# Gating's rows turned by pairs of 64-row transposes beside attention's last values, and mixing laid out by token blocks

## The chip, the cores and the metric

The kernel runs on one core of a Trainium2 chip (trn2). The metric is the device time of one execution in microseconds, as the median of three runs; beside the runs, one more execution was taken with the hardware profiler, and all rows come from it.

## What is computed

One layer of a streaming encoder for 320 tokens: 256 of a new stream ("prompt") and 64 that continue a running one ("sample"). What matters here is the gating group (gMLP) and where it stands:

```python
z = rmsnorm(x, ln_g) @ w_in                  # q, k, v and zs
a_o = attention(q, k, v)                     # 16 heads of 64, windows of chunks of 64
a = gelu(zs); u, v = a[..., :1024], rmsnorm(a[..., 1024:], g)
# mixing: 8 channel groups of 128; over blocks of 128 tokens (sample: one block of 64)
sp = einsum('gij,bnjgc->bnigc', masked(w_s), v.reshape(b, nb, 128, 8, 128)) + b_s.T[:, :, None]
s_o = u * sp                                 # gate
x = x + concat(rmsnorm(a_o), rmsnorm(s_o)) @ w_out
x = x + square(relu(rmsnorm(x) @ w_up)) @ w_down
```

The sample's normalised v rows are an output too (`sgu_v`).

## The kernel before

All activations stand transposed: channels on the 128 partitions, the 320 tokens along the free axis. Every big product runs in `products`: its weights come in tiles of 512 KB (four rows of 128 by 256 columns), ScalarE rounds a tile to `w_hi` (L115), VectorE makes the rest `w_lo` (L116), and TensorE runs 24 matmuls of 320 columns on it (L141, three for each of eight 128x128 blocks). One tile with its 24 matmuls is called a piece here; a column block of 256 of the input projection has four pieces. `w_hi` and `w_lo` have three buffers each, so ScalarE and VectorE may be up to three pieces ahead.

Work that is not a big product is put between two pieces: `between_pieces={k: f}` runs f's code after piece k, and `issue_after` with the list `narrow` (the last small matmul) sets that the next piece's matmuls follow f's on TensorE. For the rest a scheduler chooses the order on each engine; each engine then runs its own list in order and waits on semaphores.

The last column blocks of the input projection (g = 0 to 3, `u_pieces`) hold, between their pieces: attention's last three steps (`attend(10)`, `(11)`, `(12)`; each `attend` turns probabilities, computes scores, and computes the values of an earlier block, L485, in 64x64 quarters of the array), the gating rows' mean squares (`rows_norm`: three matmuls, L166, with the squares of 128 tokens as weights and one moving column; then VectorE's L169 and POOL's L171 give `rs_rows`), `by_rows` (transposes of v into rows of tokens, L553, evicted by ScalarE with the rows' norm as scale, L555) and `spatial` (mixing, L566 and L569, and VectorE's sums with the bias, L571 and L575, into `gv`). `gate` (L594) then multiplies by u.

The gated input v lies in `gv` (128 channels of group g, 320 tokens), its sample part also in `gvs`. Rows of tokens go to `vnat` (two blocks of the prompt, 0 and 1) and, for the sample (called the third block or t = 2 here), back into `gvs`' memory, `vnat_s`: there group 2a+x of token t stands on partition 64x + t, so that one matmul with a block-diagonal weight (`wsd`) mixes two groups.

PSUM's small banks: two of the tag `misc`, which every caller takes in rotation, and two score banks (`s_ps`, also taken as `g_ps`, `q0_ps` and so on). `banks(n)` gives the two misc banks and then the two score banks. A bank is written again only when its last reader is done. In `attend(12)` no probabilities are turned any more, so it takes two score banks and no misc bank.

Of the kernel before, what the change touches and what calls it, by code (L numbers as in the profile page):

```python
# [11 lines left out]
AF = mybir.ActivationFunctionType  # L12
ALU = mybir.AluOpType
AX = mybir.AxisListType

P = 128
T = 320
TP = 384
TT = [(0, 128), (128, 128), (256, 64)]
# [7 lines left out]
HD = 64  # L27
# [3 lines left out]
def hymba_step_kernel(ctx: ExitStack, tc: tile.TileContext, i, o):  # L31
    nc = tc.nc
# [12 lines left out]
    def misc():  # L45
        return ps_m.tile([P, 512], F32, name="misc", tag="misc")

    def score_bank(p, name="s_ps"):
        return ps_sc.tile([P, 512], F32, name=f"{name}{p}", tag=f"s{p}")
# [10 lines left out]
    cols = const.tile([P, 58], F32, name="cols")  # L60
# [14 lines left out]
    ident = const.tile([P, P], F32, name="ident")  # L75
# [6 lines left out]
    for _ in range(4):  # L82
        nc.tensor.matmul(out=warm_ps[:, 0:256], lhsT=nc.const_aps.tensor(0.0, [P, P], F32),  # L83
                         rhs=nc.const_aps.tensor(0.0, [P, 256], F32), start=True, stop=True)
# [255 lines left out]
    def banks(n, skip=0):  # L340

        return [misc() if x < 2 else score_bank(3 - x, "g_ps") for x in range(skip, skip + n)]
# [111 lines left out]
                                            op=ALU.mult).ins]  # L454
        probs[u] = s

    def attend(i):

        t, v = i - 2, i - 3
        t, v = t if 0 <= t < 10 else None, v if 0 <= v < 10 else None  # L460
        bank = [misc(), misc()] if t is not None else None
        s_ps = [score_bank(p) for p in range(2)]

        def behind(mms):
            with tc.issue_after(narrow[-1]):
                narrow.append([mm() for mm in mms][-1].ins)

        if t is not None:
            s = probs.pop(t).rearrange("x p j k -> x p (j k)")
            nk = blocks[units[t][0]][2]  # L470
            cols = ((P, 2),) if nk == HD else ((0, 0), (192, 1)) if nk == P else ((0, 0), (256, 1), (P, 2))
            behind([lambda p=p, x=x, c=c: nc.tensor.transpose(out=bank[p][:, x * P:(x + 1) * P], in_=s[:, p, c:c + P],  # L472
                                                              identity=ident) for p in range(2) for c, x in cols])
        if i < 10:
            behind([lambda: scores(i, s_ps)])
        if v is not None:
            blk_, kv = units[v]
            q0, va, vb = (blocks[blk_][x] for x in (0, 4, 5))
            hs = [slice(r * HD, (r + 1) * HD) for r in range(2)]
            side = {(r, j): bank[r][:, 384:512] if bank and j == 0 else s_ps[r][:, 384:512] if j else s_ps[r][:, 0:P]  # L480
                    for r in range(2) for j in range(2)}

            def part(r, j, p, span):
                lhsT, c = (va[j][hs[r], kv], slice(j * P, (j + 1) * P)) if span < 2 else (vb[j][hs[j], kv], slice(256, 384))
                return nc.tensor.matmul(out=side[r, j][hs[p]], lhsT=lhsT, rhs=pts[v % 2][p][hs[r], c],  # L485
                                        start=span < 2 or va is None, stop=span == 2 or vb is None or r != j)

            turns = [x for x in (0, 2, 1) if (va, va, vb)[x] is not None]
            behind([lambda r=r, p=p, x=x: part(r, 1 - r if x == 1 else r, p, x) for x in turns for r in range(2) for p in range(2)])
        if i < 10:  # L490
            softmax(i, s_ps)
        if v is not None:
            for j in range(2):
                dst = ao[:, 4 * kv + 2 * j:4 * kv + 2 * j + 2, q0:q0 + 64]
                nc.scalar.activation(out=dst, in_=side[j, j].rearrange("p (a q) -> p a q", a=2), func=AF.Copy)
                if va is not None:
                    nc.vector.tensor_tensor(out=dst, in0=dst, in1=side[1 - j, j].rearrange("p (a q) -> p a q", a=2), op=ALU.add)
        if t is not None:
            for p in range(2):
                c = slice(min(x for _, x in cols) * P, (max(x for _, x in cols) + 1) * P)  # L500
                nc.vector.tensor_copy(out=pts[t % 2][p][:, c], in_=bank[p][:, c])

    q3_ps = product(w_in, 0, KT, 768, xh, xl,
                    between_pieces={1: lambda: attend(0), 3: lambda: attend(1)})
# [39 lines left out]
    vnat_s = gvs.rearrange("p a t -> p (a t)")  # L544
    rv = []

    def by_rows(*ths):

        for (t, h), vps in zip(ths, banks(len(ths))):
            t0, n = TT[t]  # L550
            for a in range(4):
                cols = gv[:, 4 * h + a, t0:t0 + n] if t < 2 else gvs[:, 2 * a:2 * a + 2].rearrange("p x t -> p (x t)")
                mm = nc.tensor.transpose(out=vps[:, a * P:(a + 1) * P], in_=cols, identity=ident)  # L553
            dst = vnat[:, t, h * 512:(h + 1) * 512] if t < 2 else vnat_s
            nc.scalar.activation(out=dst, in_=vps, func=AF.Copy, scale=rv[0][:, t:t + 1])  # L555
        narrow.append(mm.ins)
        if ths[-1][0] == 2:
            for x in range(2):
                nc.gpsimd.dma_start(out=o["sgu_v"].rearrange("t (a x c) -> x t a c", a=4, x=2)[x],
                                    in_=vnat_s[x * HD:(x + 1) * HD].rearrange("t (a c) -> t a c", a=4))  # L560

    def spatial(*gs, skip=0):
        for g, sp_ps in zip(gs, banks(len(gs), skip)):
            cs = slice(g * P, (g + 1) * P)
            for b in range(2):
                nc.tensor.matmul(out=sp_ps[:, b * P:(b + 1) * P], lhsT=vnat[:, b, cs], rhs=wsT[:, g], start=True,  # L566
                                 stop=True)
            if g % 2 == 0:
                mm = nc.tensor.matmul(out=sp_ps[:, 256:384], lhsT=vnat_s[:, g // 2 * P:(g // 2 + 1) * P],  # L569
                                      rhs=wsd[:, g // 2], start=True, stop=True)  # L570
            nc.vector.tensor_tensor(out=gv[:, g, 0:256].rearrange("p (b i) -> p b i", b=2),  # L571
                                    in0=sp_ps[:, 0:256].rearrange("p (b i) -> p b i", b=2),
                                    in1=sgb[:, g, None, :].to_broadcast([P, 2, P]), op=ALU.add)
            if g % 2 == 0:
                nc.vector.tensor_tensor(out=gv[:, g:g + 2, 256:T], in0=sp_ps[:, 256:384].rearrange("p (x i) -> p x i", x=2),  # L575
                                        in1=sgb[:, g:g + 2, 0:HD], op=ALU.add)
        narrow.append(mm.ins)

    def rows_norm():
        rv.append(rstd_rows(acc_v, inv_1k, 4 * EPS))  # L580
# [2 lines left out]
    parts_a, rm_a = [], rstd_b("rm_a")  # L583
    u_pieces = {
        0: {1: lambda: attend(10), 3: lambda: attend(11)},
        1: {1: lambda: (rows_norm(), attend(12), by_rows((0, 0))), 2: lambda: by_rows((1, 0), (0, 1), (1, 1), (2, 0)),
            3: lambda: spatial(0, 1, 2, 3)},
        2: {1: lambda: spatial(4, 5, 6, 7)},
        3: {1: lambda: rstd(tuple(parts_a), mean_1k, EPS, rm_a)}}
    gus = {}  # L590

# [158 lines left out]
```

## Time and profile before

| what | value |
|---|---|
| median of 3 runs | 1239.58 us (1239.25 to 1239.84) |
| the profiled execution | 1239.04 us |
| its span, first to last instruction | 1237.3 us |
| TensorE matmul | 1232.8 us busy, 8666 records |
| VectorE, ScalarE, POOL | 663.6, 492.0, 114.0 us busy |
| granted TensorE clock over the span | 1.000 |
| the stage that changes | about 175.7 to 198.3 us of the span |

How to read it: PE is TensorE's matmuls, PEld its weight loads, DVE VectorE, ACT ScalarE, POOL GpSimd, SP the engine that issues loads. Matmuls are pipelined, so a record is longer than the distance to the next one: distances between starts tell what a matmul costs. A float32 matmul shows as two records, a transpose or a float32r matmul as one. In the chain, a piece stands by its end; in timelines by its start, so the two differ by a constant of 0.1 to 0.2 us.

### The profile page before, as it was taken

The page shows a single profiled execution, that of the slowest core. Times are in us where ns is not written, and L with a number is a line of the kernel's source. Part 1 is how long each engine was busy: PE and PEld are TensorE (multiplying, and loading weights), DVE is VectorE, ACT ScalarE, POOL GpSimd, SP SyncE. Part 2 cuts the span into 40 slices and gives each one's busy share as a digit, 9 for nine tenths or more (in the row PEclk, how much of TensorE's full clock was granted, in tenths as well). Part 3 has the DMA queues.
Part 4 walks back from the last instruction along what each step waited for, and adds up shares of the span by engine and source line. Part 5 has one row for each costly group of instructions (what it writes and reads, how often), then busy time and mean ns, then how long its engine had stood idle before and what let it go on. Part 6 is the DMA issues. An engine that isn't in the chain of part 4 may idle for free.

```text
span 1237.3 us, 20626 instructions
## 1 busy us (share of the span) xinstructions
PE 1232.8 (100%) x8666; PEld 1225.0 (99%) x8666; DVE 663.6 (54%) x796; ACT 492.0 (40%) x652; POOL 114.0 (9%) x139
## 2 busy tenths in 40 slices
PE   9999999999999999999999999999999999999998
PEld 9999999999999999999999999999999999999998
DVE  7877778877864444444444444444444434444343
ACT  7446566435534432333434332344432333433321
POOL 3127454102200000000000000000000000000000
PEclk9999999999999999999999999999999999999999
DMA  9753346444555444454444444455444454445540
GB/s 282 226 148 104 104 138 195 153 154 141 151 152 153 153 147 145 152 154 149 146 149 153 154 150 143 151 154 152 147 147 151 154 151 144 150 152 164 172 161 33
DMA packets 187934, 188.03 MB, mean 152 GB/s; under 512 B 7616, under 2 KB 187376, under 8 KB 187840
## 3 DMA queue, kind: packets, MB, share of 16 engines
q1 hardware_dynamic: 186544, 185.48, 48.7%
q0 software_dynamic: 864, 0.98, 0.4%
q8 instruction: 68, 1.11, 0.4%
q10 hardware_dynamic: 432, 0.24, 0.1%
q14 instruction: 26, 0.21, 0.1%
HBM read 183.10 MB, written 3.35 MB: 151 GB/s over the span
## 4 chain that ended last, share of the span: by engine, by line
PE 99%; DVE 0%; issue 0%; ACT 0%; DVEq 0%
PE acc L141 93%; PE q_ps L237 1%; PE misc L141 1%; PE acc L237 1%; PE s_ps L420 1%; PE misc L472 0%; PE misc L83 0%; PE misc L485 0%; PE s_ps L485 0%; PE g_ps L566 0%; PE misc L566 0%; PE misc L553 0%; PE misc L323 0%; ACT s L449 0%; ACT w_hi L115 0%
## 5 line engine op out<-in xcount | busy, mean ns | idle before, releaser
L116 DVE TENSOR_TENSOR w_lo<-w_raw,w_hi 128x1024 fp32r<-128x1024 f32 x332 | 416.0, 1253 | 422.7 <-ACT w_hi L115 414.1
L115 ACT ACTIVATE w_hi<-w_raw 128x1024 fp32r<-128x1024 f32 x332 | 351.8, 1060 | 670.9 <-PE acc L141 646.7
L141 PE MATMUL acc<-H2H,w_lo 128*128 128x320 f32 x1024 | 316.4, 309 | 0.0
L141 PE MATMUL acc<-H2H,w_hi 128*128 128x320 f32 x1024 | 316.4, 309 | 0.0
L141 PE MATMUL acc<-H2L,w_hi 128*128 128x320 f32 x1024 | 316.4, 309 | 0.0
L141 PE MATMUL acc<-FH,w_hi 128*128 128x320 f32 x992 | 306.5, 309 | 0.0
L141 PE MATMUL acc<-FL,w_hi 128*128 128x320 f32 x992 | 306.5, 309 | 0.0
L141 PE MATMUL acc<-FH,w_lo 128*128 128x320 f32 x992 | 306.5, 309 | 0.0
L141 PEld LDWEIGHTS acc<-H2H,w_hi 128*128 128x128 f32 x1024 | 192.2, 188 | 0.0
L141 PEld LDWEIGHTS acc<-H2L,w_hi 128*128 128x128 f32 x1024 | 192.2, 188 | 0.0
L141 PEld LDWEIGHTS acc<-H2H,w_lo 128*128 128x128 f32 x1024 | 192.2, 188 | 0.0
L141 PEld LDWEIGHTS acc<-FH,w_hi 128*128 128x128 f32 x992 | 186.2, 188 | 0.0
L141 PEld LDWEIGHTS acc<-FL,w_hi 128*128 128x128 f32 x992 | 186.2, 188 | 0.0
L141 PEld LDWEIGHTS acc<-FH,w_lo 128*128 128x128 f32 x992 | 186.2, 188 | 0.0
L141 PE MATMUL acc<-XH,w_hi 128*128 128x320 f32 x352 | 110.7, 314 | 0.0
L141 PE MATMUL acc<-XH,w_lo 128*128 128x320 f32 x352 | 108.8, 309 | 0.0
L141 PE MATMUL acc<-XL,w_hi 128*128 128x320 f32 x352 | 108.7, 309 | 0.0
L141 PEld LDWEIGHTS acc<-XH,w_hi 128*128 128x128 f32 x352 | 66.1, 188 | 3.1 <-issue 3.0
L141 PEld LDWEIGHTS acc<-XL,w_hi 128*128 128x128 f32 x352 | 66.1, 188 | 0.0
L141 PEld LDWEIGHTS acc<-XH,w_lo 128*128 128x128 f32 x352 | 66.1, 188 | 0.0
L658 DVE SCALAR_TENSOR_TENSOR tf<-acc,r 128x640 f32<-128x640 f32 x32 | 26.4, 824 | 41.8 <-PE acc L141 41.8
L673 DVE TENSOR_TENSOR xT<-xT,acc 128x640 f32<-128x640 f32 x31 | 25.5, 821 | 41.8 <-PE acc L141 41.8
(227 smaller groups left out, 1086.3 us busy)
## 6 DMA issues: line engine op xcount, KB each, us to landing
w_raw<-in_w_up SPq DMA_DIRECT2D x128, 512.0 KB
w_raw<-in_w_down SPq DMA_DIRECT2D x128, 512.0 KB
w_raw<-in_w_in SPq DMA_DIRECT2D x44, 512.0 KB
w_raw<-in_w_out SPq DMA_DIRECT2D x32, 512.0 KB
w_first<-in_w_in SPq DMA_DIRECT2D x14, 256.0 KB
out_yT<-xT SPq DMA_DIRECT2D x7, 320.0 KB
xT<-in_xT SPq DMA_DIRECT2D x8, 160.0 KB
xT<-in_xT SPq DMA_DIRECT2D x4, 320.0 KB
```

What stands on the lines that cost most here:

```text
L115: return (pin(nc.scalar.activation(out=hi, in_=raw, func=AF.Copy)).ins, pin(nc.vector.tensor_tensor(out=lo, in0=raw, in1=hi.bitcast(F32), ...
L116: pin(nc.vector.tensor_tensor(out=lo, in0=raw, in1=hi.bitcast(F32), op=ALU.subtract)).ins)
L141: mm = nc.tensor.matmul(out=out, lhsT=w_[:, k, g * P:(g + 1) * P], rhs=r_(kk), start=(kk == 0 and x == 0), stop=(kk == nk - 1 and x == 2))
L237: mm = nc.tensor.matmul(out=ps[:, 0:T], lhsT=w_[:, j, k, g * P:(g + 1) * P], rhs=r_(a + k), start=(a + k == 0 and x == 0), stop=(a + k == ...
L420: mm = nc.tensor.matmul(out=s_ps[p][x * HD:(x + 1) * HD, j * nk:(j + 1) * nk], lhsT=qT[hs, blk_, a + x], rhs=kz[hs, kv, k0:k0 + nk], start ...
L658: nc.vector.scalar_tensor_tensor(out=t, in0=ps[:, :, 0:T], scalar=0.0, in1=r2[:, None, :].to_broadcast([P, 2, T]), op0=ALU.max, op1=ALU.mult)
L673: nc.vector.tensor_tensor(out=xT[:, a, c], in0=xT[:, a, c], in1=p, op=ALU.add)
```

## The change

The diff, with what it does:

```diff
-    def attend(i):
+    def attend(i, beside=None):
...
+        if beside:
+            with tc.issue_after(narrow[-1]):
+                after = beside(s_ps)
         if i < 10:
             behind([lambda: scores(i, s_ps)])
...
+        if beside:
+            after()
...
-    def by_rows(*ths):
-        for (t, h), vps in zip(ths, banks(len(ths))):
-            t0, n = TT[t]
-            for a in range(4):
-                cols = gv[:, 4 * h + a, t0:t0 + n] if t < 2 else gvs[:, 2 * a:2 * a + 2].rearrange("p x t -> p (x t)")
-                mm = nc.tensor.transpose(out=vps[:, a * P:(a + 1) * P], in_=cols, identity=ident)
-            dst = vnat[:, t, h * 512:(h + 1) * 512] if t < 2 else vnat_s
-            nc.scalar.activation(out=dst, in_=vps, func=AF.Copy, scale=rv[0][:, t:t + 1])
+    def by_rows(t, *spans):
+        for a0, n, vps in spans:
+            for a in range(a0, a0 + n):
+                cols = gv[:, a, t * P:(t + 1) * P]
+                mm = nc.tensor.transpose(out=vps[:, (a - a0) * P:(a - a0 + 1) * P], in_=cols, identity=ident)
         narrow.append(mm.ins)
-        if ths[-1][0] == 2:
+        rows = vnat[:, t]
+        for a0, n, vps in spans:
+            nc.scalar.activation(out=rows[:, a0 * P:(a0 + n) * P], in_=vps[:, 0:n * P], func=AF.Copy, scale=rv[0][:, t:t + 1])
+
+    def by_halves(t, n, vps):
+        for a in range(n):
             for x in range(2):
...
+                hs = slice(x * HD, (x + 1) * HD)
+                cols = gv[hs, a, t * P:(t + 1) * P] if t < 2 else gvs[hs, 2 * a:2 * a + 2].rearrange("p x t -> p (x t)")
+                mm = nc.tensor.transpose(out=vps[x][:, a * HD:(a + 1) * HD], in_=cols, identity=ident[hs, hs])
+        narrow.append(mm.ins)
+        def out():
+            rows = (vnat[:, t] if t < 2 else vnat_s).rearrange("p (a x c) -> p x a c", a=n, x=2)
+            for x in range(2):
+                nc.scalar.activation(out=rows[:, x], in_=vps[x].rearrange("p (a c) -> p a c", a=n), func=AF.Copy,
+                                     scale=rv[0][:, t:t + 1])
...
+        return out
+
+    def first_rows(s_ps):
+        rows_norm()
+        outs = [by_halves(2, 4, [s_ps[x][:, P:384] for x in range(2)]), by_halves(0, 8, [misc() for _ in range(2)])]
+        return lambda: [out() for out in outs]
+
+    def sample_mix():
+        sp_ps = misc()
+        for a in range(4):
+            mm = nc.tensor.matmul(out=sp_ps[:, a * P:(a + 1) * P], lhsT=vnat_s[:, a * P:(a + 1) * P], rhs=wsd[:, a],
+                                  start=True, stop=True)
+        narrow.append(mm.ins)
+        nc.vector.tensor_tensor(out=gv[:, :, 256:T], in0=sp_ps.rearrange("p (g i) -> p g i", g=8), in1=sgb[:, :, 0:HD],
+                                op=ALU.add)
+
+    def mix():
+        for x, sp_ps in enumerate(banks(4)):
+            b, gs = x // 2, slice(x % 2 * 4, x % 2 * 4 + 4)
+            for y in range(4):
+                g = x % 2 * 4 + y
+                mm = nc.tensor.matmul(out=sp_ps[:, y * P:(y + 1) * P], lhsT=vnat[:, b, g * P:(g + 1) * P], rhs=wsT[:, g],
+                                      start=True, stop=True)
+            nc.vector.tensor_tensor(out=gv[:, gs, b * P:(b + 1) * P], in0=sp_ps.rearrange("p (g i) -> p g i", g=4),
+                                    in1=sgb[:, gs], op=ALU.add)
+        narrow.append(mm.ins)
...
     u_pieces = {
         0: {1: lambda: attend(10), 3: lambda: attend(11)},
-        1: {1: lambda: (rows_norm(), attend(12), by_rows((0, 0))), 2: lambda: by_rows((1, 0), (0, 1), (1, 1), (2, 0)),
-            3: lambda: spatial(0, 1, 2, 3)},
-        2: {1: lambda: spatial(4, 5, 6, 7)},
+        1: {1: lambda: attend(12, first_rows),
+            2: lambda: (by_rows(1, *((4 * x, 4, score_bank(x, "g_ps")) for x in range(2))), sample_mix()), 3: mix},
```

`spatial` goes. Before, attend(12) was followed by four full transposes of block 0, the next gap had sixteen (the rest of both blocks and the sample's four), and two gaps had mixing by groups. After, attend(12) has the mean squares, eight half transposes of the sample (into the free columns of the two score banks) and sixteen of block 0 (into the two misc banks) ahead of its values; the next gap has block 1's eight full transposes and the sample's mixing, the third gap all the mixing of the prompt by block and half of the groups. A half transpose takes the 64 channels on one half of the partitions; the two halves of a group go to two banks. Their evictions (`out`) come after the values' in the code. VectorE's sums are five instead of twelve. The new function's lines are L569 (half transposes), L575 (their evictions), L557 and L561 (full transposes and evictions), L592 and L595 (the sample's mixing and sum), L603 and L605 (the prompt's); attention's values (L485) are L488 there, their evictions (L495, L497) L498 and L500, and the gate (L594) is L623.

On TensorE, in the gap with attend(12), behind the three matmuls of the mean squares (the numbers at the names tell buffers of one name apart; misc_2282 is the bank of the mean squares). Before:

```order
L166 MATMUL misc_2282<-inv_1k_104,acc_v_1056 128x1 x3
L485 MATMUL s_ps0_2290<-pt1_868,kzv_465 64x128 x2
L485 MATMUL s_ps1_2291<-pt1_868,kzv_465 64x128 x2
L485 MATMUL s_ps0_2290<-pt1_868,kzv_465 64x128 x2
L485 MATMUL s_ps1_2291<-pt1_868,kzv_465 64x128 x2
L485 MATMUL s_ps0_2290<-pt1_868,kzv_465 64x128 x2
L485 MATMUL s_ps1_2291<-pt1_868,kzv_465 64x128 x2
L553 MATMUL misc_2308<-ident_89,gv_1055 128x128 x4
```

And after, from the third pair of the sample's half transposes on (two pairs stand ahead, and ahead of them the mean squares into misc_2284):

```order
L569 MATMUL s_ps0_2282<-ident_89,gvs_1057 128x64
L569 MATMUL s_ps1_2283<-ident_89,gvs_1057 128x64
L569 MATMUL s_ps0_2282<-ident_89,gvs_1057 128x64
L569 MATMUL s_ps1_2283<-ident_89,gvs_1057 128x64
L569 MATMUL misc_2300<-ident_89,gv_1055 128x64 x8
L569 MATMUL misc_2301<-ident_89,gv_1055 128x64 x8
L488 MATMUL s_ps0_2282<-pt1_868,kzv_465 64x128 x2
L488 MATMUL s_ps1_2283<-pt1_868,kzv_465 64x128 x2
```

The sample's halves alternate; block 0's do not, although the code writes them in turn: eight of the first half stand ahead of eight of the second, which write misc_2301, the bank that misc_2284 had (the tag has two). The values stand behind all of them.

On VectorE, around the reader of the mean squares (`r_rows`). Before:

```order
L524 SCALAR_TENSOR_TENSOR gu_2212<-gc_2215,z_2213 128x640
L116 TENSOR_TENSOR w_lo_2372<-w_raw_2370,w_hi_2371 128x1024
L206 SCALAR_TENSOR_TENSOR AL_2211<-ao_86,cols_82,AH_2210 128x320
L169 TENSOR_SCALAR r_rows_2286<-misc_2282 128x3
L116 TENSOR_TENSOR w_lo_2456<-w_raw_2454,w_hi_2455 128x1024
```

After:

```order
L529 SCALAR_TENSOR_TENSOR gu_2212<-gc_2215,z_2213 128x640
L116 TENSOR_TENSOR w_lo_2390<-w_raw_2388,w_hi_2389 128x1024
L206 SCALAR_TENSOR_TENSOR AL_2211<-ao_86,cols_82,AH_2210 128x320
L169 TENSOR_SCALAR r_rows_2288<-misc_2284 128x3
L116 TENSOR_TENSOR w_lo_2478<-w_raw_2476,w_hi_2477 128x1024
```

Nothing moved here: a weight half and a split of attention's output stand ahead of it in both.

On ScalarE, in the same gap, from one weight tile's high half to the next. Before:

```order
L115 ACTIVATE w_hi_2455<-w_raw_2454 128x1024
L495 ACTIVATE ao_86<-s_ps0_2290 128x2x64
L495 ACTIVATE ao_86<-s_ps1_2291 128x2x64
L555 ACTIVATE vnat_867<-misc_2308,rs_rows_2288 128x512
L115 ACTIVATE w_hi_2485<-w_raw_2484 128x1024
```

After:

```order
L115 ACTIVATE w_hi_2477<-w_raw_2476 128x1024
L575 ACTIVATE vnat_867<-misc_2300,rs_rows_2290 128x8x64
L575 ACTIVATE vnat_867<-misc_2301,rs_rows_2290 128x8x64
L498 ACTIVATE ao_86<-s_ps0_2282 128x2x64
L498 ACTIVATE ao_86<-s_ps1_2283 128x2x64
L575 ACTIVATE gvs_1057<-s_ps1_2283,rs_rows_2290 128x4x64
L575 ACTIVATE gvs_1057<-s_ps0_2282,rs_rows_2290 128x4x64
L115 ACTIVATE w_hi_2507<-w_raw_2506 128x1024
```

Block 0's evictions, which need the row norms, now stand ahead of those of attention's values, and the sample's behind them.

More of the change, by code (lines that the diff above doesn't have):

```diff
@@ L545, in hymba_step_kernel @@
     rv = []
-    def by_rows(*ths):
-        for (t, h), vps in zip(ths, banks(len(ths))):
-            t0, n = TT[t]
-            for a in range(4):
-                cols = gv[:, 4 * h + a, t0:t0 + n] if t < 2 else gvs[:, 2 * a:2 * a + 2].rearrange("p x t -> p (x t)")
-                mm = nc.tensor.transpose(out=vps[:, a * P:(a + 1) * P], in_=cols, identity=ident)
-            dst = vnat[:, t, h * 512:(h + 1) * 512] if t < 2 else vnat_s
-            nc.scalar.activation(out=dst, in_=vps, func=AF.Copy, scale=rv[0][:, t:t + 1])
-        narrow.append(mm.ins)
-        if ths[-1][0] == 2:
-            for x in range(2):
-                nc.gpsimd.dma_start(out=o["sgu_v"].rearrange("t (a x c) -> x t a c", a=4, x=2)[x],
-                                    in_=vnat_s[x * HD:(x + 1) * HD].rearrange("t (a c) -> t a c", a=4))
@@ L562, in spatial @@
[L562 to L576, printed above, removed]
+    def by_rows(t, *spans):
[3 more added lines that the diff above has]
+                mm = nc.tensor.transpose(out=vps[:, (a - a0) * P:(a - a0 + 1) * P], in_=cols, identity=ident)
+        narrow.append(mm.ins)
+        rows = vnat[:, t]
+        for a0, n, vps in spans:
+            nc.scalar.activation(out=rows[:, a0 * P:(a0 + n) * P], in_=vps[:, 0:n * P], func=AF.Copy, scale=rv[0][:, t:t + 1])
@@ new lines, in by_halves @@
+    def by_halves(t, n, vps):
+        for a in range(n):
+            for x in range(2):
+                hs = slice(x * HD, (x + 1) * HD)
[7 more added lines that the diff above has]
+                                     scale=rv[0][:, t:t + 1])
+                if t == 2 and x == 1:
+                    for y in range(2):
+                        nc.gpsimd.dma_start(out=o["sgu_v"].rearrange("t (a x c) -> x t a c", a=4, x=2)[y],
+                                            in_=vnat_s[y * HD:(y + 1) * HD].rearrange("t (a c) -> t a c", a=4))
+        return out
```

## The prediction

> **What bounds the kernel now.** I read the page's busy times, then the list of what TensorE waited for, then the chain that ended last around the change, and then the engines' timelines there.
>
> ```profile
> PE 1232.8 (100%) x8666; PEld 1225.0 (99%) x8666; DVE 663.6 (54%) x796; ACT 492.0 (40%) x652; POOL 114.0 (9%) x139
> PE 99%; DVE 0%; issue 0%; ACT 0%; DVEq 0%
> PE misc L472 <- DVE vnat L501: 0.3, 1, 0.3
> ```
>
> TensorE is busy all the time, the chain runs through it from end to end, and in the whole kernel it waits for another engine's work once, for 0.3 us. So what TensorE issues is the time, and each wait that the change gives it is added to the end in full. The chain through the stage that changes (start, us, what):
>
> ```profile
> 176.03 0.56 PE misc L166 x6
> 176.60 0.82 PE s_ps L485 x24
> 177.41 0.59 PE misc L553 x4
> 178.00 3.51 PE acc L141 x24
> 181.51 0.87 PE misc L553 x8
> 182.39 0.87 PE g_ps L553 x8
> ...
> 186.77 0.89 PE misc L566 x8
> ...
> 189.00 7.04 PE acc L141 x48
> 196.04 0.44 PE misc L566 x4
> ```
>
> L141 is the projection; between its pieces stand the sums of squares (L166), attention's last values (L485), the row transposes (L553) and the mixing (L566, L569). A full transpose takes 0.87 / 8 = 0.109 us, a mixing matmul two records of 0.89 / 8 = 0.111. A mixing group has 20 records: 189.00 - 186.77 = 2.23.
>
> **The change, costed.** First the work that is only recounted. The third block's transposes and those of block 0 leave the full form (4 + 8 = 12 of 20): -12 x 0.109 = -1.31 us. Mixing keeps 20 matmuls, 40 records in both; eight now stand with block 1's transposes, 32 in one group, at the same 0.111: 0. Instead come 24 half transposes, 64 rows in and 64 columns through. Their price is not in this trace. Lowest: two halves side by side, each half as long as a full one, 0.027 a half. Highest: each as long as a full one, 0.109. The nearest rows are the scores, which also move 64 columns from 64 rows (chain; 64, 128 and 192 columns):
>
> ```profile
> 70.79 0.39 PE s_ps L420 x16
> 78.42 0.60 PE s_ps L420 x16
> 86.47 0.81 PE s_ps L420 x16
> ```
>
> Sixteen records in four rounds of four: 64 columns more cost a round (0.60 - 0.39) / 4 = 0.053 us, which is half of 0.109. And four matmuls on different quarters do start together:
>
> ```profile
> 167.91 0.32 PE L485 MATMUL misc<-kzv 64*64 64x128 f32 x1
> ...
> 167.94 0.32 PE L485 MATMUL s_ps<-vnat,kzv 64*64 64x128 f32 x1
> ```
>
> So I take 0.055 for a half among others of the same partitions, and 0.055 for two halves of different partitions that alternate. In the order of the instructions only the third block's eight alternate (4 x 0.055 = 0.22); block 0's stand as eight of one half, then eight of the other (16 x 0.055 = 0.88). Sum for the halves: +1.10 (0.66 to 2.6).
>
> A change of array shape costs something: from the projection to the scores the starts lie 70.72 - 70.48 = 0.24 apart, where projection starts lie 3.51 / 24 = 0.15 apart.
>
> ```profile
> 70.48 0.31 PE L141 MATMUL acc<-XH,w_lo 128*128 128x320 f32 x1
> 70.72 0.46 PE L420 MATMUL s_ps<-kzv,qT 64*64 64x64 f32 x16
> ```
>
> The halves add one such change, to the values behind them: +0.09 (0 if the values share their shape, 0.18 if both ends pay).
>
> Now the wait that is new. Block 0's second eight write the `misc` bank that rows_norm's sums (L166) have just used (there are two, taken in rotation); VectorE must read that bank first (L169). Who stands ahead of L169 on VectorE, and what TensorE does meanwhile:
>
> ```profile
> 176.02 1.23 DVE L116 TENSOR_TENSOR w_lo<-w_raw,w_hi 128x1024 fp32r<-128x1024 f32 x1
> 177.16 1.16 DVE L206 SCALAR_TENSOR_TENSOR AL<-ao,cols,AH 128x320 fp32r<-128x320 f32 x1
> 178.25 0.15 DVE L169 TENSOR_SCALAR r_rows<-misc 128x3 f32<-128x3 f32 x1
> 175.87 0.72 PE L166 MATMUL misc<-inv_1k,acc_v 128*128 128x1 f32 x6
> 176.53 0.89 PE L485 MATMUL s_ps<-pt,kzv 64*64 64x128 f32 x24
> 177.34 0.66 PE L553 MATMUL misc<-ident,gv 128*128 128x128 f32 x4
> 177.76 0.39 PE L141 MATMUL acc<-XH,w_hi 128*128 128x320 f32 x1
> ```
>
> The sums are done long before VectorE gets to them; L169 ends at 178.25 + 0.15 = 178.40, and nothing ahead of it there moves with the change (the rows of VectorE are the same in both). In the kernel before nobody on TensorE asks for that bank before the transposes at 181.51, so it cost nothing. What TensorE needs to start after such a wait is in the one wait of the trace:
>
> ```profile
> 166.78 0.55 DVE L501 COPY vnat<-misc 128x384 f32<-128x384 f32 x1
> 167.47 0.52 PE L472 MATMUL misc<-ident,s 128*128 128x128 f32 x3 [0.34 <-DVE vnat L501]
> ```
>
> 167.47 - (166.78 + 0.55) = 0.14. So, by starts: halves begin at 176.53, where the values began; 0.22 and 0.44 bring 177.19; the second eight can begin at 178.40 + 0.14 = 178.54: a wait of 1.35 us. Behind it on TensorE are the values and the next projection piece. The second eight end at 178.98, the values start at 179.07 and take 177.34 - 176.53 = 0.81 as before; the projection goes on at 179.88 instead of 177.76, 2.12 later. Then block 1 has 8 transposes where 16 stood (-0.87), the third block's mixing 8 records (+0.89), the mixing 32 records where 40 stood (-0.89).
>
> 2.12 - 0.87 + 0.89 - 0.89 = **+1.25 us**; by kinds: -1.31 + 1.10 + 0.09 + 1.35 = 1.23, the same within rounding. Of the halves' own bounds only the last eight count, since the first sixteen run into the wait: at 0.027 it would be +1.03, at 0.109 +1.68.
>
> What else moves, and is hidden. ScalarE's two evictions of block 0 now stand ahead of the values' evictions (L495) and wait for POOL's power (L171):
>
> ```profile
> 178.47 1.79 POOL L171 TENSOR_TENSOR rs_rows<-r_rows,nhalf 128x3 f32<-128x3 f32 x1 [0.50 <-DVE r_rows L169]
> 179.75 0.28 ACT L495 ACTIVATE ao<-s_ps 128x128 f32<-128x128 f32 x1 [1.85 <-DVE ao L497]
> 180.30 0.69 ACT L555 ACTIVATE vnat<-misc,rs_rows 128x512 f32<-128x512 f32 x1 [0.27 <-POOL rs_rows L171]
> ```
>
> From 180.30: two of 0.69, two of 0.28, two of 256 columns at about 0.42 (between 0.28 for 128 and 0.69 for 512) end by 183.1. Block 1's transposes want these banks at 179.88 + 3.51 = 183.4, and the mixing of the third block after that: 0.3 us to spare. If that is gone, each 0.1 us of ScalarE is 0.1 us of TensorE. The output DMA on POOL's queue goes earlier, and the load queue on SP keeps its order: 0.
>
> The profiled execution took 1239.04 us (span 1237.3), so 1240.3 for it; the runs' median lies 0.54 higher, 1239.58 + 1.26 = **1240.8**.
>
> **The rivals.**
> *The halves are bound by their weight load* and cost 0.109 each. For it: L166 moves a single column and still takes 0.56 / 6 = 0.093 a record. Against it: the loads of the transposes are recorded shorter than those of L166, and nearly as short as 64-column loads (min/median/max ns):
>
> ```profile
> L553 PEld LDWEIGHTS misc<-ident,gv x12: 139/141/142, 177.3 to 182.0; 128*128 128x128 f32 x12
> L166 PEld LDWEIGHTS misc<-inv_1k,acc_v x6: 187/192/192, 175.7 to 176.3; 128*128 128x128 f32 x6
> L420 PEld LDWEIGHTS s_ps<-kzv,qT x160: 129/133/135, 70.7 to 149.9; 64*64 64x64 f32 x160
> ```
>
> The first sixteen then end by 176.53 + 1.75 = 178.28, still before 178.54; only the last eight add 8 x 0.054 = 0.43: +1.68, 1241.3. [...]
>
> *The wait does not bite.* If VectorE read the sums before L206, at 177.25, the second eight could start at 177.25 + 0.15 + 0.14 = 177.54: 1.00 us less, +0.25; if it never mattered, 1.25 - 1.35 = -0.10: 1239.5 to 1239.8. For it: L169 depends on nothing later than L166. Against it: the order puts L206 and its 1.16 us ahead.
>
> *Weight halves come late.* VectorE now waits for the whole mixing, then runs two gates in a row, and ScalarE takes their squares and copies ahead of the next w_hi. Before, this part was early by much:
>
> ```profile
> 198.27 14.08 PE acc L141 x96
> 199.06 1.37 DVE L116 TENSOR_TENSOR w_lo<-w_raw,w_hi 128x1024 fp32r<-128x1024 f32 x1
> 191.43 2.09 DVE L594 SCALAR_TENSOR_TENSOR gv<-gv,gu 128x640 f32<-128x640 f32 x1
> 193.88 0.46 ACT L509 ACTIVATE acc_s<-gv 128x320 f32<-128x320 f32 x1
> ```
>
> This w_lo is ready at 200.43 for the piece at 198.27 + 7.04 = 205.31: 4.9 us early. Now mixing ends near 179.88 + 3.51 + 1.76 + 3.51 + 3.55 = 192.2; the last sum (0.7) and the first gate (2.1) bring VectorE to 195.0, six squares and copies and a tanh at about 0.5 ScalarE to 198.5, w_hi and w_lo (1.06 and 1.37) 200.9, for the piece at 192.2 + 3 x 3.52 = 202.8: some 2 us are left. It decides if those slip; say 1.0 us on top, 1241.8.
>
> *Slower: the clock falls while TensorE waits.* The trace has a slow TensorE once, at its start: four records in 1.34 us, then 0.58.
>
> ```profile
> 4.57 1.34 PE q_ps L237 x4
> 5.91 0.58 PE acc L237 x4
> ```
>
> If 1.35 us without work brought back such a spell of 5 us at 0.58 / 1.34 of the speed, 5 x (1 - 0.43) = 2.8 us would be lost: +4.1, 1243.7. Against it: the wait at 167 is followed by no slower record. It decides where an idle spell between 0.3 and 1.35 us is enough.
>
> **How the numbers follow.** Forecast (wait of 1.35, halves at 0.055): 0.62. Load-bound halves: 0.17. No wait: 0.08. Late weights: 0.08. Clock: 0.05. A measurement of this kernel can tell about 0.2% from no change, 2.5 us. Forecast, load-bound halves, missing wait and most of late weights lie inside; the clock case and a worse lateness are slower, 0.07; nothing here gives 2.5 us back, since all 24 halves and the wait for nothing would be -1.31, so faster is 0.01, same 0.92. The range 1239.7 to 1241.9 holds the forecast, the load-bound halves (1241.3), late weights and the upper end of the missing wait.
>
> **What will show it.** Right: TensorE waits once more, some 1.3 us, its second eight halves (L569) released by L169 on VectorE; the third block's halves start in pairs; block 0's halves about 0.055 apart; the piece behind attend(12) starts near 179.9, the mixing is one group of 3.55 us, and from 200 us on every row stands 1.2 to 1.3 us later. Wrong: halves 0.11 apart (load), no wait at L569, waits of L141 for w_lo around 200 to 206, L141 records further than 0.147 apart after 178.5 (clock), or waits at L557 for ScalarE's evictions.

## The result: a wait as forecast, and a clock that was not

In 21 executions the changed kernel took 1242.08 us in the median (1240.49 to 1244.08), the kernel before 1239.6 (1238.89 to 1240.82, 21 executions): a ratio of 1.0021, 95% interval 1.0014 to 1.0027. That is +2.5 us where +1.25 was forecast, above the range's upper end of 1241.9. The median hides two groups. Nine executions list a mean granted clock of 1.000 and took 1240.49 to 1241.77; twelve list 0.999 or less and took 1241.87 to 1244.08. The profiled execution (1241.19 us, span 1239.4) is one of the first group.

Its page's busy times, and the list of what TensorE waited for (engine, line, what released it; us in total, times, longest):

```profile
PE 1233.4 (100%) x8678; PEld 1224.8 (99%) x8678; DVE 664.3 (54%) x789; ACT 491.8 (40%) x653; POOL 116.7 (9%) x139
```
```profile
PE misc L569 <- DVE r_rows L169: 1.3, 1, 1.3
...
PE misc L472 <- DVE vnat L504: 0.3, 1, 0.3
```

One wait is new, at the forecast place and from the forecast releaser. The chain round it (start us, us, what):

```profile
177.31 0.65 issue
177.96 1.15 DVE AL L206
179.12 0.08 DVE r_rows L169
179.20 0.04 issue
179.24 0.71 PE misc L569 x8
179.95 0.82 PE s_ps L488 x24
180.77 3.71 PE acc L141 x24
184.48 0.87 PE g_ps L557 x8
185.36 0.89 PE misc L592 x8
186.25 3.52 PE acc L141 x24
189.77 1.78 PE misc L603 x16
191.56 1.79 PE g_ps L603 x16
```

In the kernel before, the chain ran through TensorE all through this stage; here it leaves TensorE and runs through VectorE. The timeline shows the wait itself, and that POOL's sum of squares (L518) lies beside L206:

```profile
176.93 0.46 PE L569 MATMUL s_ps<-ident,gvs 64*128 64x64 f32 x8
...
177.23 0.66 PE L569 MATMUL misc<-ident,gv 64*128 64x64 f32 x8
...
177.74 1.03 POOL L518 TENSOR_TENSOR acc_a<-acc_a,sq 128x320 f32<-128x320 f32 x1 [2.67 <-ACT sq L517]
177.96 1.15 DVE L206 SCALAR_TENSOR_TENSOR AL<-ao,cols,AH 128x320 fp32r<-128x320 f32 x1
...
179.04 0.15 DVE L169 TENSOR_SCALAR r_rows<-misc 128x3 f32<-128x3 f32 x1
...
179.24 0.71 PE L569 MATMUL misc<-ident,gv 64*128 64x64 f32 x8 [1.35 <-DVE r_rows L169]
```

How much of a difference belongs to the changed stage can be read from two rows of each trace: the projection piece ahead of the stage, and TensorE's last record (before, then after, of both):

```profile
159.49 0.41 PE L141 MATMUL acc<-XH,w_hi 128*128 128x320 f32 x1
...
1233.69 0.31 PE L141 MATMUL misc<-FH,w_lo 128*128 128x320 f32 x1
```
```profile
159.90 0.41 PE L141 MATMUL acc<-XH,w_hi 128*128 128x320 f32 x1
...
1235.80 0.31 PE L141 MATMUL misc<-FH,w_lo 128*128 128x320 f32 x1
```

Ahead of the stage the profiled executions differ by 0.41 us, at the end by 2.11, so the stage itself costs 1.70. What differs ahead of 159 us lies ahead of the changed instructions; over all profiles below it is 0.07 to 1.18 us, a part of the scatter of the times. Behind the stage nothing more is gained or lost: from 210 us to the end each profile keeps its difference. The column "stage" below is this difference, worked out in the same way for each profile.

### The profile page after: what moved, and what is told of

It reads as the page before. It is cut to its first block, busy times and chain, and to the rows that moved or that the text cites. A ratio compares the mean times of both kernels' runs of the same rounds, so it can differ in the third digit from the quotient of the medians.

```text
span 1239.4 us, 20642 instructions
## 1 busy us (share of the span) xinstructions
PE 1233.4 (100%) x8678; PEld 1224.8 (99%) x8678; DVE 664.3 (54%) x789; ACT 491.8 (40%) x653; POOL 116.7 (9%) x139
## 3 DMA queue, kind: packets, MB, share of 16 engines
q8 instruction: 68, 1.11, 0.4%
## 4 chain that ended last, share of the span: by engine, by line
PE 96%; DMA 2%; DVE 1%; issue 1%; SPq 0%; ACT 0%; DVEq 0%; ACTq 0%
PE acc L141 93%; DMA xT<-in_xT 1%; PE misc L141 1%; PE s_ps L420 1%; SPq L110 0%; PE misc L472 0%; DVE ssq L290 0%; PE misc L488 0%; PE s_ps L488 0%; DVE w_lo L116 0%; DMA kzv<-in_cv 0%; PE g_ps L603 0%; PE misc L603 0%; ACT w_hi L115 0%; PE misc L323 0%
## 5 line engine op out<-in xcount | busy, mean ns | idle before, releaser
L116 DVE TENSOR_TENSOR w_lo<-w_raw,w_hi 128x1024 fp32r<-128x1024 f32 x332 | 417.6, 1258 | 421.2 <-ACT w_hi L115 412.6
L141 PE MATMUL acc<-H2H,w_lo 128*128 128x320 f32 x1024 | 316.4, 309 | 0.0
L141 PE MATMUL acc<-H2L,w_hi 128*128 128x320 f32 x1024 | 316.4, 309 | 0.0
L141 PE MATMUL acc<-H2H,w_hi 128*128 128x320 f32 x1024 | 316.4, 309 | 0.0
L141 PE MATMUL acc<-FH,w_hi 128*128 128x320 f32 x992 | 306.5, 309 | 0.0
L141 PE MATMUL acc<-FL,w_hi 128*128 128x320 f32 x992 | 306.5, 309 | 0.0
L141 PE MATMUL acc<-FH,w_lo 128*128 128x320 f32 x992 | 306.5, 309 | 0.0
L141 PEld LDWEIGHTS acc<-H2H,w_hi 128*128 128x128 f32 x1024 | 192.2, 188 | 0.0
L141 PEld LDWEIGHTS acc<-H2H,w_lo 128*128 128x128 f32 x1024 | 192.2, 188 | 0.0
L141 PEld LDWEIGHTS acc<-H2L,w_hi 128*128 128x128 f32 x1024 | 192.2, 188 | 0.0
L141 PEld LDWEIGHTS acc<-FH,w_hi 128*128 128x128 f32 x992 | 186.2, 188 | 0.0
L141 PEld LDWEIGHTS acc<-FL,w_hi 128*128 128x128 f32 x992 | 186.2, 188 | 0.0
L141 PEld LDWEIGHTS acc<-FH,w_lo 128*128 128x128 f32 x992 | 186.2, 188 | 0.0
L141 PE MATMUL acc<-XH,w_hi 128*128 128x320 f32 x352 | 110.6, 314 | 0.0
L141 PE MATMUL acc<-XH,w_lo 128*128 128x320 f32 x352 | 108.8, 309 | 0.0
L141 PE MATMUL acc<-XL,w_hi 128*128 128x320 f32 x352 | 108.7, 309 | 0.0
L141 PEld LDWEIGHTS acc<-XH,w_hi 128*128 128x128 f32 x352 | 66.1, 188 | 3.3 <-issue 3.0
L141 PEld LDWEIGHTS acc<-XL,w_hi 128*128 128x128 f32 x352 | 66.1, 188 | 0.0
L141 PEld LDWEIGHTS acc<-XH,w_lo 128*128 128x128 f32 x352 | 66.1, 188 | 0.0
```

What stands on the lines that cost most here:

```text
L116: pin(nc.vector.tensor_tensor(out=lo, in0=raw, in1=hi.bitcast(F32), op=ALU.subtract)).ins)
L141: mm = nc.tensor.matmul(out=out, lhsT=w_[:, k, g * P:(g + 1) * P], rhs=r_(kk), start=(kk == 0 and x == 0), stop=(kk == nk - 1 and x == 2))
```

## The experiments

Theory A: the wait at L569 is the loss, and its idleness also makes TensorE's clock fall in part of the executions, which costs them more than the wait. Theory B: the clock falls because of the halves or the mixing layout. One table has all kernels. The kernel before was run beside each: it had 1239.42 us (22 executions) beside the early sums, the overfilled wait, the kernel before with a wait and the longer wait, 1239.56 (21) beside POOL's sum later and all halves, and 1239.85 (33) beside the others. In the code cuts below, `...` stands for lines left out.

| kernel | median us (range, executions) | lists a clock under 1.000 | stage, us |
|---|---|---|---|
| changed, again | 1241.28 (1240.92 to 1243.42, 11) | 5 | 2.88 |
| sums early | 1239.51 (1238.69 to 1241.02, 11) | 0 | -0.24 |
| wait overfilled | 1242.71 (1242.29 to 1244.47, 9) | 0 | 3.16 |
| wait filled | 1241.15 (1240.73 to 1241.91, 11) | 1 | 1.82 |
| before, with a wait | 1242.97 (1241.59 to 1243.71, 8) | 5 | 3.67 |
| longer wait | 1244.40 (1243.59 to 1245.0, 5) | 5 | 5.08 |
| sums read first | 1240.22 (1239.38 to 1241.05, 11) | 0 | 0.24 |
| POOL's sum later | 1241.25 (1239.97 to 1242.67, 11) | 3 | 1.11 |
| mixing alone | 1239.81 (1238.98 to 1241.09, 11) | 1 | 0.00 |
| all halves | 1239.69 (1239.11 to 1239.91, 11) | 1 | -0.04 |

A listed 0.999 is no proof by itself: 8 of the 76 executions of the kernel before list it too. In the trace of the early sums the clock also fell when TensorE had run out of work at the very end (to 0.50 at 1236.9 us, 2.2 us behind the last matmul), which may be why. Proof is a spell in a trace: a stretch at half clock while TensorE works.

**The changed kernel again.** Nothing is edited.

> The changed kernel itself, next to the others on one chip. Theory A: two groups of times, some 1.7 to 2.0 us apart (1241.2 and 1243.1), about half of the executions in each; where the profiled execution is of the later group, a spell of 3.4 us at half clock begins within 3.4 us behind the wait's start at 177.7 us. Theory B: the same groups, the spell elsewhere.

This profile (1242.51 us) is of the later group. Windows of its trace, cut where its clock changes (from:to, length, busy us of PE, PEld, DVE, ACT, POOL with counts, granted clock, DMA share, GB/s), and its chain:

```profile
176.32:179.73 3.41, 2.46 (x36) 2.24 (x39) 3.29 (x5) 2.00 (x4) 1.72 (x2) 1.00 0.16 29
179.73:183.14 3.41, 3.41 (x31) 3.08 (x32) 0.83 (x3) 1.93 (x5) 1.09 (x1) 0.50 0.85 256
183.14:186.56 3.42, 3.42 (x27) 3.41 (x27) 0.10 (x1) 1.41 (x3) 1.31 (x2) 1.00 0.42 94
```
```profile
179.01 0.71 PE misc L569 x8
179.72 1.47 PE s_ps L488 x24
181.19 4.63 PE acc L141 x24
```

The stretch of 3.41 us that holds the wait has 3.41 - 2.46 = 0.95 us without TensorE work; the next one is granted half the clock, though TensorE works all through it, and then the clock is back. The values take 1.47 instead of 0.82, the projection piece 4.63 instead of 3.71: 1.57 us, near half of 3.41. (The stage is only 1.18 us longer than in the first profile, since the wait is 0.40 shorter.) The place is the one that theory A named. Together the 32 executions of the changed kernel have medians of 1241.13 us at clock 1.000 (15) and 1243.0 below it (17): 1.9 apart.

Why only in half of them? In the traces the recorded clock first rises 4.3 to 6.2 us into the program, and its later changes lie whole multiples of 3.413 us behind that. In the kernel before the one later change comes 1232.21 us behind the rise, in the first profile of the changed kernel 1235.63, one step of 3.41 more: 361 and 362 of them. The spell of this profile and those of two below begin 174.08 us behind it, 51 steps. Counted so (an estimate from these distances), the 51st step of the changed kernel's first profile ends at 4.50 + 174.08 = 178.58 us, in the middle of the wait:

```profile
175.17:178.58 3.41, 2.72 (x31) 2.57 (x29) 2.58 (x3) 3.38 (x5) 0.84 (x1) 1.00 0.00 0
178.58:181.99 3.41, 2.75 (x41) 2.51 (x42) 1.74 (x3) 0.89 (x2) 1.99 (x2) 1.00 0.67 171
```

That leaves 0.69 and 0.66 us of idleness in the two steps, and no spell. These two profiles fit one reading: what counts is how much of the wait lies in one step, and that shifts from execution to execution. For the other executions, which have no trace, it is not shown.

**Sums early: the wait taken away.** The sums go to unused columns of a score bank at the end of attend(11):

```diff
-        st = misc()                                     # rstd_rows takes st as an argument
...
+        if i == 11:                                     # in attend, behind the values
+            with tc.issue_after(narrow[-1]):
+                rows_norm(s_ps)                         # sums in s_ps[0][:, P:P + 4]
...
-        rows_norm()                                     # in first_rows
```

> The changed kernel, but rows_norm's sums are issued at the end of attend(11), one projection piece and more earlier, and into unused columns of a score bank, so that block 0's second eight halves find their bank free. Theory A (the wait at L569 is the loss, and it is also what makes the granted clock fall in part of the executions): no wait at the halves, all 24 halves in pairs, the stage shorter by the wait of 1.51 us and by about eight halves of 0.0625 (0.5): 1241.1 (the changed kernel's executions at clock 1.000) - 2.0 = 1239.1 us, and every execution at 1.000. Theory B (the halves or the mixing layout cost the clock, the wait does not): still about half of the executions at 0.999, these some 1.9 us later, median near 1240.5. Theory C (something else eats it: evictions or weights late once the wait is gone): 1239.6 or more at clock 1.000, with a new wait of TensorE between 178 and 206 us.

No wait, all executions at clock 1.000, and the halves run in pairs all through:

```profile
177.60 0.46 PE L572 MATMUL s_ps<-ident,gvs 64*128 64x64 f32 x8
177.90 0.66 PE L572 MATMUL misc<-ident,gv 64*128 64x64 f32 x16
```

The sixteen halves of block 0 take the 0.66 us that eight took before. The stage is 1.70 + 0.24 = 1.94 us shorter than the changed kernel's, as theory A has it (2.0). The gain of 0.24 over the kernel before shows in the stage alone: the ratio is 0.9999, interval 0.999 to 1.0008.

**The wait filled.** Twelve, then six products by the identity between the two eights:

```diff
+                if t == 0 and (x, a) == (1, 0):
+                    with tc.issue_after(mm.ins):
+                        for y in range(FILL):           # 12, then 6
+                            mm = nc.tensor.matmul(out=free[y % 2][:, 0:P], lhsT=ident, rhs=gv[:, y % 8, 0:P], start=True, stop=True)
...
```

The lines left out fix block 0's order as the changed kernel has it: eight of the first half, the products, eight of the second.

> The changed kernel, with twelve products of 128x128 by the identity between block 0's first and second eight halves, written to columns of the score banks that the values overwrite later: TensorE works through most of the 1.5 us that it waited, and starts the second eight when it did. Theory A (idleness makes the clock fall): the same times of start as in the changed kernel, all executions at clock 1.000, median 1241.2 us with a spread of about 1 us, none above 1242.3. Theory B (halves or layout cost the clock): about half of the executions at 0.999, up to 1244, median near 1242. If the twelve take longer than the wait, up to 0.2 us more in either.

> The changed kernel with six products between block 0's first and second eight halves instead of the twelve of the run before: twelve took 24 records of 0.112 = 2.7 us and overran the wait, six take 1.34 and fit into its 1.51. Theory A (idleness makes the clock fall): TensorE's starts behind the halves as in the changed kernel, no half-speed spell, every execution in one group round 1241.2 us. Theory B (halves or layout cost the clock): two groups as in the changed kernel, round 1241.2 and 1243.2, median near 1242.

Twelve were too many: they are 24 records, 2.7 us, and the stage is 1.46 us longer than the changed kernel's (3.16 against 1.70), where I had allowed for 0.2. None of the nine executions lists a clock under 1.000, but their times, up to 1244.47, can't be compared with theory A's. Six fit. The window that holds the former wait, in the second run:

```profile
176.70:180.11 3.41, 3.41 (x52) 3.15 (x55) 2.93 (x4) 1.17 (x2) 2.56 (x2) 1.00 0.43 108
```

TensorE is busy throughout, the end is as late as with the wait (stage 1.82 against 1.70), and the later group is gone: 1240.73 to 1241.91, median 1241.15, that of the changed kernel at clock 1.000 (one execution lists 0.999, at 1241.86). Halves and layout are the changed kernel's, the times of start too but for 0.1 us. Theory B falls.

**A wait in the kernel before.** No halves, the old mixing; the first four transposes are put ahead of attend(12) and into the sums' own bank:

```diff
-        for (t, h), vps in zip(ths, banks(len(ths))):
+        for (t, h), vps in zip(ths, banks(len(ths)) if len(ths) > 1 else rv[1:]):   # rv[1] is the sums' bank
...
-        1: {1: lambda: (rows_norm(), attend(12), by_rows((0, 0))),
+        1: {1: lambda: (rows_norm(), by_rows((0, 0)), attend(12)),
```

> The kernel before, with block 0's first four transposes put ahead of attend(12) and into the bank of the sums: no halves and no new mixing, only a wait for L169 that should last some 2.0 us (the sums end near 176.4, L169 near 178.4). Theory A: 1239.6 + 2.0 = 1241.6 in the executions at clock 1.000, and half or more at 0.999, some 1.9 us later, so a median of 1242.5 to 1243.6. Theory B: 1241.6 in all executions, clock 1.000.

Two executions are at 1241.6, which is the expected 2.0 us of the wait alone, and six are from 1242.64 to 1243.71; five of these six list a clock under 1.000, the lowest does not. The profiled one (1243.18, a wait of 1.8 us) is of the five:

```profile
175.50:178.91 3.41, 1.56 (x14) 1.48 (x13) 3.29 (x5) 2.62 (x4) 1.09 (x2) 1.00 0.02 7
178.91:182.33 3.42, 3.42 (x32) 2.76 (x33) 1.27 (x2) 1.24 (x3) 1.73 (x1) 0.50 0.79 223
```
```profile
178.82 1.07 PE misc L555 x4
179.90 1.49 PE s_ps L487 x24
181.38 4.17 PE acc L142 x24
```

A step with 3.41 - 1.56 = 1.85 us without TensorE work is followed by one at half clock, and four full transposes take 1.07 us where before eight took 0.87. The wait alone, without halves or the new mixing, is enough.

**A longer wait.** Three copies on VectorE read the sums ahead of L169:

```diff
+        slow = sums("slow")
+        for _ in range(3):
+            nc.vector.tensor_copy(out=slow[:, :, None], in_=st[:, 0:1, None].to_broadcast([P, T, 1]))
```

> The changed kernel, with three copies of 320 columns on VectorE that read the sums ahead of L169; a weight half of 1.2 us falls between them in VectorE's order, so that the wait at L569 grows from 1.5 to about 4 us. Theory A: the wait's own growth of 2.6 us in every execution, and the clock falls in nearly all of them: median 1241.1 + 2.6 + 2 to 4 = 1245.7 to 1247.7, with clocks of 0.997 to 0.999. Theory B (the wait costs no clock): 1241.1 + 2.6 = 1243.7 where the clock is 1.000, half of the executions at 0.999 as without it.

The wait grew less than both theories were told, to 2.3 us. The split (L209 here) took 0.55 us instead of 1.15, and the weight half ahead of it began 1.0 us earlier against TensorE than in the first profile of the changed kernel (176.09 with the piece at 160.19, against 176.82 with 159.90):

```profile
177.24 0.55 DVE L209 SCALAR_TENSOR_TENSOR AL<-ao,cols,AH 128x320 fp32r<-128x320 f32 x1
...
178.26 2.72 POOL L521 TENSOR_TENSOR acc_a<-acc_a,sq 128x320 f32<-128x320 f32 x2 [3.92 <-ACT acc_a L517]
```
```profile
175.84:179.26 3.42, 2.35 (x29) 2.20 (x27) 3.30 (x6) 2.34 (x5) 1.00 (x1) 1.00 0.17 31
179.26:182.67 3.41, 2.21 (x32) 2.09 (x32) 1.02 (x4) 0.00 (x0) 3.25 (x4) 0.50 0.85 265
182.67:186.08 3.41, 3.41 (x20) 3.12 (x13) 0.58 (x2) 2.54 (x6) 0.19 (x2) 0.50 0.06 18
186.08:189.49 3.41, 3.41 (x28) 3.40 (x28) 0.31 (x1) 1.40 (x2) 1.20 (x2) 1.00 0.37 77
```

The wait reaches into two steps (1.07 and 1.20 us idle), and two steps are at half clock. All five executions are later than any of the changed kernel's at clock 1.000, and four list 0.997. The median of 1244.40 lies under theory A's 1245.7 to 1247.7, which was worked out with a wait of 4 us.

**The sums read first.** L169 ahead of L206 in VectorE's order:

```diff
-            with tc.issue_after(high), tc.issue_after(low):
+            with tc.issue_after(high), tc.issue_after(rests[-1] if (g, x) == (1, 2) else low):   # rests[-1]: L169
```

> The changed kernel, with VectorE's reading of the sums (L169) put ahead of the split L206 in its order: L169 can then start when the weight half L116 is done, at 177.96 instead of 179.04, so the wait shrinks from 1.51 to about 0.5 us. Theory A: 1241.2 - 1.0 = 1240.2, and the clock falls seldom or never with 0.5 us of idleness, so one group of times. Theory B: two groups 1.9 us apart, round 1240.2 and 1242.1.

```profile
176.11 1.23 DVE L116 TENSOR_TENSOR w_lo<-w_raw,w_hi 128x1024 fp32r<-128x1024 f32 x1
177.25 0.15 DVE L169 TENSOR_SCALAR r_rows<-misc 128x3 f32<-128x3 f32 x1
177.32 1.09 DVE L206 SCALAR_TENSOR_TENSOR AL<-ao,cols,AH 128x320 fp32r<-128x320 f32 x1
```

L169 starts 1.14 us after L116 does, as expected; but VectorE as a whole stands 0.4 us earlier against TensorE than in the first profile of the changed kernel (L116 0.7 earlier, the piece at 159 us 0.3), and so the wait of 0.5 that I expected is gone altogether. One group of times, all at clock 1.000; stage +0.24. That the prediction gave +0.25 for VectorE reading first is luck: its sum still held a wait of 0.35 us there, and without one it gave -0.10; here there is no wait, and the halves with the steps between their groups took 1.48 us where 1.19 had been counted. Against the changed kernel at clock 1.000 the median falls from 1241.13 to 1240.22: one line of order takes back 0.9 us and every later execution.

**POOL's sum later.** L206 takes 1.15 us ahead of L169, and 0.55 in the longer wait, where POOL's sum starts after it.

```diff
...
-                add_square(acc_a, ao[:, a], a == 0)
+                add_square(acc_a, ao[:, a], a == 0, rests[-1] if g == 1 and a > 2 else None)   # behind rs_rows on POOL
```

> The changed kernel, with one addition of squares on POOL (acc_a, 1.03 us, which overlaps L206 on VectorE) put behind the power of the sums in POOL's order; VectorE's order stays. Theory D (L206 takes 1.15 us ahead of L169, where it takes 0.54 elsewhere, because POOL works at that time): L206 takes 0.55, L169 comes 0.6 us earlier, the wait shrinks from 1.51 to 0.9: 1241.2 - 0.6 = 1240.6 us. With theory A the clock falls in few executions or none, since a window then holds no more idleness (0.7 us) than the undisturbed profile of the changed kernel had in one. Rival: L206 takes 1.15 whatever POOL does (its operands), the wait stays at 1.2 to 1.5 and two groups of times remain, 1241.2 and 1243.

```profile
178.75 0.55 DVE L206 SCALAR_TENSOR_TENSOR AL<-ao,cols,AH 128x320 fp32r<-128x320 f32 x1
...
179.21 0.15 DVE L169 TENSOR_SCALAR r_rows<-misc 128x3 f32<-128x3 f32 x1
...
179.42 0.71 PE L570 MATMUL misc<-ident,gv 64*128 64x64 f32 x8 [0.74 <-DVE r_rows L169]
```
```profile
175.97:179.39 3.42, 2.71 (x31) 2.55 (x29) 2.61 (x5) 3.36 (x5) 0.00 (x0) 1.00 0.00 1
```

Theory D holds in the trace: L206 takes 0.55, the idleness shrinks from 1.35 to 0.74, the stage by 0.59. In this execution 0.71 us of it lie in one step, and no spell follows. The times don't settle the clock: 1239.97 to 1241.34 in seven, 1241.91 to 1242.67 in four, with a median of 1241.25 against 1240.6 expected. Three of the four list 0.999, the latest 1.000; whether they had a spell no trace shows.

The end of the same trace shows that idleness alone does not decide:

```profile
1234.11:1237.52 3.41, 2.17 (x15) 1.91 (x14) 1.04 (x3) 0.00 (x0) 0.00 (x0) 1.00 0.14 48
1237.52:1239.56 2.04, 0.00 (x0) 0.00 (x0) 0.00 (x0) 0.00 (x0) 0.00 (x0) 1.00 0.26 80
```

The step in which the last matmul ends has 1.24 us without TensorE work, more than the 0.95 of the changed kernel's wait, and yet the next step has the whole clock. In the same place 1.05 us (wait overfilled) and 1.03 us (longer wait) were followed by the whole clock too, 2.20 us (sums early) by half of it. TensorE's work in these last steps is matmuls of 320 columns; the steps with the wait also hold one-column sums and halves. What a step counts, no run here shows.

**Mixing alone**, put into the kernel before:

```diff
...
-            3: lambda: spatial(0, 1, 2, 3)},
-        2: {1: lambda: spatial(4, 5, 6, 7)},
+            3: lambda: (sample_mix(), mix())},
```

> The kernel before with its full transposes and its order of the first rows, but with the new mixing: the third block's mixing and one group for the two blocks. The prediction's recount says 0 for TensorE: 1239.5 us, one group of times. If the layout were what costs, 1240.5 or more; if a projection waits for weight halves behind the longer VectorE work, a wait at L141 after 195 us.

Stage 0.00, no wait behind it: the recount of the mixing at nothing was right.

**All halves: the version the runs point to.** Sums early, and block 1 by halves as well.

```diff
...
-            2: lambda: (by_rows(1, *((4 * x, 4, score_bank(x, "g_ps")) for x in range(2))), sample_mix()), 3: mix},
+            2: lambda: (by_halves(1, 8, [score_bank(x, "g_ps") for x in range(2)])(), sample_mix()), 3: mix},
```

> The version that the runs point to: the sums early as in the run that took the wait away, and block 1's eight transposes also as sixteen halves in alternating pairs. Theory A: that run's traces put its stage 0.24 us under the kernel before, once what differs ahead of it is taken off. Eight pairs of 0.0625 for eight transposes of 0.109 give 0.37 back, a first gap of 0.109 and one more change of array shape cost about 0.15: a stage 0.45 us under the kernel before, 1239.3 us, which the timing alone will hardly tell from the 1239.8 of before; no wait, clock 1.000. Rival: block 1's evictions, now strided, hold up the mixing: a wait at L603 of some tenths, 1239.8 or more.

Not as expected: the ratio is 0.9999 (0.999 to 1.0007), the stage -0.04 instead of -0.45. The chain tells why:

```profile
182.50 0.89 PE g_ps L572 x16
183.39 1.09 PE misc L595 x8
```

The halves did not alternate throughout: in the trace four pairs start within 0.01 us of each other, and the other eight halves start alone. So sixteen halves take 0.89 us where eight full transposes took 0.87. The change of shape is paid at both ends: by starts 0.24 us from the projection to the halves instead of 0.15, and 0.21 between the first two of the mixing instead of 0.11. Together that is the 0.20 us by which this stage lies above that of the early sums. No version measurably beats the kernel before; the best stage is that of the early sums, 0.24 us under it.

## Why the prediction was wrong

The step that failed is the rival on the clock, which the sum put at nothing. I gave it a chance of 0.05, because nothing slow followed the wait at 167 us, and priced it at 2.8 us on top by the slow start. Its mechanism came true: one of two traces of the changed kernel has the spell, and 17 of 32 executions list the lower clock, 1.9 us later in the median. The wait at 167 could not speak against it: with 0.34 us it is shorter than all that was followed by a spell. For the new wait the traces put the point between 0.71 and 0.95 us of idleness in one step of the clock, with a single profile at each end; at the end of the program 1.24 us were not enough, so that it is no general measure. The price failed too: I let the slow start stand for the spell's length (5 us) and speed (0.43), and a spell is one step of 3.41 us at 0.50, 1.7 us. With the forecast's own wait that is 1240.8 + 1.7 = 1242.5, and a range up to there would have held the median.

Point by point, for the execution at clock 1.000 (1.70 us forecast as 1.25; times of the changed kernel less the 0.41 us from ahead):

- **The wait**: right in place, releaser and cause, +1.35 forecast. By starts it was 179.24 - 177.73 = 1.51 here and 1.11 in the second profile, since VectorE is later against TensorE by a few tenths in one execution than in another. Second eight: 178.83 instead of 178.54, +0.29.
- **A half transpose**: 0.063 between starts, (0.66 - 0.22) / 7 with 0.22 for one record, and 0.11 for the first of a group, where I took 0.055 from the scores: +0.11 on the last eight. Pairs cost the same as single ones, as forecast. The load-bound rival (0.109) is refuted.
- **Change of array shape**: I charged one (0.09), and one came: 0.154 from the last half to the values, where halves follow each other at 0.063. The projection behind the values starts almost as it did behind the full transposes, its first two starts 0.25 apart (180.70, 180.95) against 0.23 (177.76, 177.99): +0.02.
- **The rest** (fewer full transposes, mixing moved and regrouped) came out 0.03 higher than forecast: 0.29 + 0.11 + 0.02 + 0.03 = 0.45.
- **Evictions and late weights**: no wait at L557, none at L141 behind the change. The rival of late weights is refuted.
- **L206**: I took its 1.16 us as its own length and did not ask why it was twice that of its shortest rows (0.54); with POOL's sum put behind, it took 0.55, so 0.6 us of the wait are POOL's.
- **The chain of the kernel before**: it does not run through TensorE from end to end, as I wrote; from 161.6 to 167.5 us, ahead of its one wait, it lies on ScalarE and VectorE. The sum does not use this.

At clock 1.000 the 15 executions' median of 1241.13 lies 0.3 above the forecast and inside its range. What took the measured time out of the range is the clock alone: with the same starts and TensorE kept busy the median was 1241.15.

## What to carry to other kernels

A wait of TensorE that nothing hid had two prices here: its length, and half a clock step, 1.7 us, for each step in which 0.95 us or more of it fell; price a new wait of a microsecond with both, and look at the clock listed for each execution before trusting one profile. Before a bank is given a second user, ask which instruction frees it and what stands ahead of that one on its engine: here the order of two VectorE instructions was worth 0.9 us, and with it went the executions at the lower clock. An instruction that takes twice its usual time on the row you build on (L206: 1.15 against 0.55 us) is a question to answer (what ran beside it?), not a duration to copy.

## What the runs showed of the hardware

- The granted clock fell to 0.50 for 3.41 us in two profiles (changed again; before, with a wait) and for 6.82 us, two steps, in a third (longer wait), right behind a step of 3.41 us with 0.95, 1.85 and 1.07 us without TensorE work; the second of the two steps stands behind one with 1.20. In two other profiles 0.66 and 0.69 us (changed) and 0.71 (POOL's sum later) did not bring it. At the end of the program 1.03, 1.05 and 1.24 us did not bring it either, so that idleness in a step does not decide alone; what else counts stays open. The three spells begin 174.08 us behind the clock's first rise, which is 51 steps of 3.413 us.
- VectorE's split L206 took 0.55 us where POOL was idle (longer wait, POOL's sum later) and 1.15 in the first profile of the changed kernel, where POOL, which began 0.22 us earlier, added squares for 1.03 us; the split ended 0.34 us after POOL did. By what means POOL's work lengthens it, no run shows.
- A transpose of 64 rows into 64 columns followed the last at 0.063 us, one by one (changed) or in pairs of different rows (sums early), against 0.109 for 128 by 128.
